# A two-layer hybrid decoder trunk on one core: memory queries produced already turned, and two output projections written in another order

## The chip, the cores and the metric

The kernel runs on one core of one Trainium2 chip. The metric is the time of one execution in microseconds (us) of device time.

## The reference, cut to what matters

256 positions of 1024 features pass through two layers. Each layer has a token mixer, a four-head cross-attention into 256 memory tokens, one output projection over both, and a SwiGLU feed-forward part (FFN) of inner width 2816, each behind an RMS norm:

```python
for i in range(2):
    h = rmsnorm(x, norm_mix[i]); mem_n = rmsnorm(mem, norm_mem[i])
    mix, mem_q = gmlp_mixer(h, ...) if i == 0 else nsa_mixer(h, ...)
    mem_o = mem_cross_attention(mem_q, mem_n, w_mem_kv[i])
    x = x + concatenate([mix, mem_o], -1) @ w_out[i]
    h = rmsnorm(x, norm_ffn[i])
    x = x + (silu(h @ wg) * (h @ wu)) @ wd
return rmsnorm(x, norm_final)

def mem_cross_attention(q, mem_n, w_kv):       # 4 heads of 64
    k, v = split(mem_n @ w_kv, 2)
    p = softmax(einsum('bshd,bmhd->bhsm', q, k) * 64 ** -0.5)
    return einsum('bhsm,bmhd->bshd', p, v)
```

Layer 0 is a gated spatial unit (`u * (w_s @ norm(v) + b)`, 12 groups). Layer 1 is a sparse attention of 12 heads with three gated branches: a compressed one (15 blocks), a selected one and a sliding one.

## The kernel before, in words

The 256 positions are two blocks `tb` of 128 rows. Every product in float32 is made of three matmuls (`mm3`, lines 229 to 231): activations and weights are each split into a high and a low part in a reduced float32, and high by high, low by high and high by low are added up in one PSUM bank. The weights stream in by DMA on the SP queue into three `raw` buffers (line 153); ACT casts the high part `wH` (L123), DVE subtracts for the low part `wL` (L124), seven buffers each. A raw buffer is loaded anew once the `wL` of its last piece is made. The same two lines split activations into `aH` and `aL`. A norm's factor per row (`rstd`) is not applied to the activations but behind the product, where it is evicted.

PE's order is written by hand. A model clock (`Flow`) advances by the length of each product, and side chains (generators that `spawn` starts and that `yield` delays) emit their transposes (L245) and small matmuls when the clock has reached them. A wait that the model clock doesn't foresee is not filled with other work: PE runs in order. ACT, DVE, POOL and the DMA queue are ordered by a scheduler with priorities; up to `early.close()` it orders them with a timeline simulation.

PSUM has four banks `mm` for projections and accumulators and four banks `tr` for transposes, scores and attention outputs. A tile named `tr` can be written only when the tile four requests earlier has been read.

*Layer 0.* Behind the gating products come, for each block, the memory queries (`WQ0`, 256 wide), scaled by `rstd` on DVE (L693) and turned by two transposes on PE (`mem_queries`, copy on L377). `mem_kv` makes the keys and values of the memory (`WK0`). Meanwhile `v_chain` makes the gated product `gm` (L673), turns it and splits it into k-tiles 0 to 5 of `mix`. `mem_attention` does for each block: scores (L389), maximum (L393, DVE), its negative scaled (`nb`, L395, POOL), four Exp (L401, ACT), division (L406, POOL), after a delay `MEMLAT` the transposes of the probabilities and their copies (L414, ACT), then the output (L422, 16 matmuls) that is split into k-tiles 6 and 7 of `mix`. The output projection (`down`) adds up k-tiles 0 to 3 of all four accumulators (two blocks, two halves), and once both memory attentions are done, 4 to 7.

*Layer 1.* Six pairs of heads `m` pass through `scores(m)` (L927 to L931; mask and row maximum on DVE, L947; eight Exp on ACT, L951; division on POOL, L956; the compressed branch's softmax in `pcx`, L961 to L967), `turn(m)` (12 transposes of probabilities, three `tr` tiles, copies on ACT, L976 and L982; then in a fourth `tr` tile the one transpose of `pcx`, copy on L985) and `attend(m)` (L1003, 32 matmuls into one `tr` tile, split into `aH`, `aL`). Between them `mixed((k, tb))` puts two products of the output projection, k-tile k of block tb. Per step m nine `tr` tiles are asked for: four by scores, four by turn, one by attend. Behind the last pieces the transposes of the new `x` (L245, `x`), their split and the FFN follow.

Of the kernel before, what the change touches and what calls it, by code (L numbers as in the profile page):

```python
# [12 lines left out]
ALU = mybir.AluOpType  # L13
# [3 lines left out]
SEQ = 256  # L17
# [6 lines left out]
SCALE = 0.125  # L24
# [35 lines left out]
HI = 150  # L60
UP = 500
MEMLAT = 9.0
# [6 lines left out]
def body(tc, t, out):  # L69
    nc = tc.nc  # L70
    PE, ACT, DVE, POOL, SP = nc.tensor, nc.scalar, nc.vector, nc.gpsimd, nc.sync
    with ExitStack() as ctx:
# [309 lines left out]
        def mem_attention(qTs, tb, kv, dst, done):  # L382
# [12 lines left out]
            POOL.tensor_scalar(nb, mx, -SCALE, None, op0=ALU.mult)  # L395
            sm = tiny([128, 4], "sm")
            parts = [small([128, 2, 256]) for _ in range(2)]
            for i in range(2):
                for j in range(2):
                    n = i * 2 + j  # L400
                    ACT.activation(parts[i][:, j, :], scs[i][:, j * 256 : (j + 1) * 256], AF.Exp, bias=nb[:, n : n + 1],  # L401
                                   scale=SCALE, accum_out=sm[:, n : n + 1])
# [247 lines left out]
        def v_chain():  # L650
# [17 lines left out]
            for c, n in ((0, 512), (512, 256)):  # L668
                for tb in range(2):
# [4 lines left out]
                    yield 1.0  # L674
# [12 lines left out]
        qT0 = [None, None]  # L687
        for tb in range(2):
            ps = mm()
            gemm(ps, n0.act, tb, WQ0, 256)  # L690
            mq = small([128, 256])
            with tc.high_priority(offset=HI):
                DVE.tensor_scalar(mq, ps[:, 0:256], n0.rstd[tb], None, op0=ALU.mult)  # L693
            flow.spawn(mem_queries(mq, tb, qT0), 1.2)
        flow.until(lambda: mem_done)
        kv0 = mem_kv(WK0)
        flow.until(lambda: None not in qT0)
        for tb in range(2):
            flow.spawn(mem_attention(qT0, tb, kv0, mix, mo_done), 1.0 + 5.5 * tb)
# [4 lines left out]
        down(accs, mix, [0, 1, 2, 3], WO0[0] + WO0[1], True, False)  # L704
        flow.until(lambda: len(mo_done) == 2)
        down(accs, mix, [4, 5, 6, 7], WO0[2] + WO0[3], False, True,
             lambda *a: flow.spawn(f0.chain(*a)))
# [262 lines left out]
        def turn(m):  # L970
# [12 lines left out]
            tc_ = tr()  # L983
            transposes(tc_, pcs[:, m % 2], 1)
            ACT.copy(pcT[:, m % 2], tc_[:, 0:128])  # L985
            turned[m] = pT0, pT1

# [30 lines left out]
        def step(f, *a):  # L1018
            with tc.high_priority(offset=UP if f is turn else HI):
                f(*a)  # L1020
# [30 lines left out]
        step(turn, 0)  # L1051
        step(scores, 2)
        step(attend, 0)
        step(turn, 1)
        mixed((0, 0))
        step(scores, 3)
        step(attend, 1)
        step(turn, 2)
        mixed((1, 0))
        step(scores, 4)  # L1060
        step(attend, 2)
        step(turn, 3)
        mixed((0, 1))
        step(scores, 5)
# [3 lines left out]
        mixed((1, 1), (3, 0))  # L1068
        step(attend, 4)
        step(turn, 5)  # L1070
        mixed((2, 1), (4, 0))
        step(attend, 5)
        mixed((3, 1), (5, 0), (4, 1), (5, 1))
# [66 lines left out]
```

## Time and profile before

| | |
|---|---|
| time, median of 3 runs | 633.94 us (633.56 to 634.37) |
| the profiled execution | 634.55 us, span 632.8 us |
| PE matmul busy | 618.1 us (98%) |
| DVE, ACT, POOL busy | 377.1, 327.3, 58.2 us |
| granted TensorE clock | 0.998 |
| HBM read | 108.07 MB, 172 GB/s over the span |

The busy share says how much of the span an engine worked. PE at 98% leaves some 15 us in which it did nothing, and the waits list says in front of which lines. In the timeline of PE the distance between the starts of neighbours is the true pace, since the ends of matmuls are modelled: 0.12 us for a matmul of 256 columns and 0.23 us for one of 512.

### The profile page before, as it was taken

The page shows a single profiled execution, that of the slowest core. Times are in us where ns is not written, and L with a number is a line of the kernel's source. Part 1 is how long each engine was busy: PE and PEld are TensorE (multiplying, and loading weights), DVE is VectorE, ACT ScalarE, POOL GpSimd, SP SyncE. Part 2 cuts the span into 40 slices and gives each one's busy share as a digit, 9 for nine tenths or more (in the row PEclk, how much of TensorE's full clock was granted, in tenths as well). Part 3 has the DMA queues.
Part 4 walks back from the last instruction along what each step waited for, and adds up shares of the span by engine and source line. Part 5 has one row for each costly group of instructions (what it writes and reads, how often), then busy time and mean ns, then how long its engine had stood idle before and what let it go on. Part 6 is the DMA issues. An engine that isn't in the chain of part 4 may idle for free.

```text
span 632.8 us, 8848 instructions
## 1 busy us (share of the span) xinstructions
PE 618.1 (98%) x3382; PEld 513.9 (81%) x3382; DVE 377.1 (60%) x616; ACT 327.3 (52%) x553; POOL 58.2 (9%) x90
## 2 busy tenths in 40 slices
PE   8999999999999999999999999899999999999995
PEld 7889879888888888889886787678988888888884
DVE  3998457464554544566688479766544645446344
ACT  4885557452534434456543559766533535344423
POOL 0330121000000000002001204431000000000001
PEclk9999999999999999999999999999999999999999
DMA  7966254555546464643967742133554655647401
GB/s 244 369 217 247 75 165 169 200 172 186 177 171 225 138 261 134 241 159 87 330 201 206 193 103 65 35 121 115 198 199 134 226 173 179 220 138 235 159 1 67
DMA packets 57331, 109.69 MB, mean 173 GB/s; under 512 B 3429, under 2 KB 19401, under 8 KB 57289
## 3 DMA queue, kind: packets, MB, share of 16 engines
q1 hardware_dynamic: 57272, 109.12, 51.9%
q8 instruction: 26, 0.43, 0.3%
q14 instruction: 17, 0.13, 0.1%
q10 hardware_dynamic: 16, 0.00, 0.0%
HBM read 108.07 MB, written 1.05 MB: 172 GB/s over the span
## 4 chain that ended last, share of the span: by engine, by line
PE 90%; ACT 5%; DVE 2%; DMA 1%; issue 1%; POOL 0%; SPq 0%; POOLq 0%; ACTq 0%; DVEq 0%
PE mm L229 14%; PE mm L230 14%; PE mm L231 14%; PE tr L230 13%; PE tr L231 13%; PE tr L229 13%; PE tr L245 5%; ACT mid L951 3%; PE tr L800 1%; DMA x<-in_x_dram 1%; PE tr L389 1%; PE tr L422 1%; PE tr L1003 1%; ACT wH L123 1%; DVE wL L124 0%
## 5 line engine op out<-in xcount | busy, mean ns | idle before, releaser
L124 DVE TENSOR_TENSOR wL<-raw,wH 128x1024 fp32r<-128x1024 f32 (+1 forms) x170 | 205.5, 1228 | 149.5 <-ACT wH L123 143.8
L123 ACT CAST wH<-raw 128x1024 fp32r<-128x1024 f32 (+1 forms) x170 | 173.8, 1043 | 152.3 <-PE tr L230 75.5
L229 PE MATMUL tr<-wH,aH 128*128 128x512 f32 (+1 forms) x384 | 143.8, 375 | 0.0
L230 PE MATMUL tr<-wH,aL 128*128 128x512 f32 (+1 forms) x384 | 142.8, 372 | 0.6 <-DVE aL L124 0.6
L231 PE MATMUL tr<-wL,aH 128*128 128x512 f32 (+1 forms) x384 | 142.7, 372 | 0.0
L229 PE MATMUL mm<-wH,aH 128*128 128x512 f32 (+2 forms) x224 | 87.7, 391 | 0.0
L230 PE MATMUL mm<-wH,aL 128*128 128x512 f32 (+2 forms) x224 | 83.2, 371 | 0.0
L231 PE MATMUL mm<-wL,aH 128*128 128x512 f32 (+2 forms) x224 | 83.2, 371 | 0.0
L230 PEld LDWEIGHTS tr<-wH,aL 128*128 128x128 f32 x384 | 72.4, 188 | 13.0 <-DVE aL L124 0.9
L231 PEld LDWEIGHTS tr<-wL,aH 128*128 128x128 f32 x384 | 72.3, 188 | 12.5
L229 PEld LDWEIGHTS tr<-wH,aH 128*128 128x128 f32 x384 | 72.3, 188 | 12.3
L229 PE MATMUL mm<-wH,mid 128*128 128x512 f32 (+1 forms) x208 | 79.2, 381 | 0.0
L230 PE MATMUL mm<-wH,mid 128*128 128x512 f32 (+1 forms) x208 | 77.9, 374 | 0.0
L231 PE MATMUL mm<-wL,mid 128*128 128x512 f32 (+1 forms) x208 | 77.8, 374 | 0.0
L229 PEld LDWEIGHTS mm<-wH,aH 128*128 128x128 f32 x224 | 42.9, 191 | 9.6 <-issue 4.0
L231 PEld LDWEIGHTS mm<-wL,aH 128*128 128x128 f32 x224 | 42.6, 190 | 7.4
L258 POOL TENSOR_SCALAR rstd<-ss 128x1 f32<-128x1 f32 x14 | 8.0, 575 | 434.6 <-ACT junk L250 430.5
L230 PEld LDWEIGHTS mm<-wH,aL 128*128 128x128 f32 x224 | 42.7, 191 | 5.6
L231 PEld LDWEIGHTS mm<-wL,mid 128*128 128x128 f32 x208 | 39.2, 188 | 7.1
L230 PEld LDWEIGHTS mm<-wH,mid 128*128 128x128 f32 x208 | 39.3, 189 | 6.8 <-DVE mid L124 0.5
L229 PEld LDWEIGHTS mm<-wH,mid 128*128 128x128 f32 x208 | 39.2, 189 | 6.7 <-ACT mid L123 0.4
L453 DVE SCALAR_TENSOR_TENSOR small<-tr,rstd,small 128x512 f32<-128x512 f32 (+1 forms) x24 | 16.9, 703 | 36.5 <-PE tr L231 36.5
(158 smaller groups left out, 652.6 us busy)
## 6 DMA issues: line engine op xcount, KB each, us to landing
raw<-in_ffn_w_down_dram SPq DMA_DIRECT2D x22, 1024.0 KB, 5.1
raw<-in_ffn_w_gate_dram SPq DMA_DIRECT2D x20, 1024.0 KB, 5.2
raw<-in_ffn_w_up_dram SPq DMA_DIRECT2D x20, 1024.0 KB, 5.1
raw<-in_nsa_w_in_dram SPq DMA_DIRECT2D x6, 1024.0 KB, 6.9
raw<-in_gmlp_w_in_dram SPq DMA_DIRECT2D x4, 1024.0 KB, 8.1
raw<-in_w_mem_kv_dram SPq DMA_DIRECT2D x4, 1024.0 KB, 5.8
raw<-in_gmlp_w_out_dram SPq DMA_DIRECT2D x4, 1024.0 KB, 6.2
raw<-in_nsa_w_out_dram SPq DMA_DIRECT2D x12, 256.0 KB, 4.9
```

Source lines behind the costliest of these rows:

```text
L123: ACT.copy(H, src)
L124: DVE.tensor_tensor(L, src, H.bitcast(F32), op=ALU.subtract)
L229: PE.matmul(ps, aH, bH, start=first, stop=False)
L230: PE.matmul(ps, aL, bH, start=False, stop=False)
L231: PE.matmul(ps, aH, bL, start=False, stop=last)
L245: PE.transpose(ps[:, (at + j) * 128 : (at + j + 1) * 128], src[:, j * 128 : (j + 1) * 128], ident)
L258: POOL.tensor_scalar(r, ss[:, 0:1], ss[:, 1:2], EPS, op0=ALU.add, op1=ALU.add)
L389: PE.matmul(scs[i][:, j * 256 : (j + 1) * 256], qT[r, j, :], kv[r, j, :], start=True, stop=True)
L422: PE.matmul(o[i * 64 : i * 64 + 64, blk(j)], kv[:, 2 + b, h : h + 64], pTs[i][:, j * 2 + b, :], start=b == 0, stop=b == 1)
L453: DVE.scalar_tensor_tensor(h, ps[:, :n], nrm.rstd[tb], sil[tb], op0=ALU.mult, op1=ALU.mult)
L800: PE.matmul(ph[s * 64 : s * 64 + 60, 0:256], X[s][:, k // 8, k % 8, :], w1[q, s][:, j, :], start=k == 0, stop=k == 15)
L951: ACT.activation(o, o, AF.Exp, bias=nb[:, i : i + 1], scale=-1.0, accum_out=sm[:, i : i + 1])
```

## The change

(a) Layer 0's memory queries are computed already turned: the weights `WQ0` are the stationary operand, and the activations of both blocks, 256 columns, move. One DVE copy (L696 of the changed kernel) evicts both blocks. The row factor is now missing in the queries; it goes into the scale of the Exp and of `nb`, as a `[128,1]` tile per block (`qs`, two tiny POOL operations each). The two scalings on L693, the four transposes and the two copies on L377 are gone. (b) `MEMLAT` is 8 for 9, the second memory attention is spawned 3.5 behind the first for 5.5, and `gm` is waited for 2.0 on the model clock for 1.0. (c) Layer 0's output projection runs k-tiles 4 and 5 of block 0 ahead of the point that asks for both memory attentions, then 6 and 7 of block 0, then 4 to 7 of block 1. (d) In layer 1 the transpose of the compressed branch is a step of its own, `turn_c`, put behind the next `mixed` for m = 1 to 5, and the last `mixed` pieces are in another order.

```diff
-MEMLAT = 9.0
+MEMLAT = 8.0
...
-            POOL.tensor_scalar(nb, mx, -SCALE, None, op0=ALU.mult)
+            POOL.tensor_scalar(nb, mx, -SCALE if scales is None else scales[tb][1], None, op0=ALU.mult)
...
                     ACT.activation(parts[i][:, j, :], scs[i][:, j * 256 : (j + 1) * 256], AF.Exp, bias=nb[:, n : n + 1],
-                                   scale=SCALE, accum_out=sm[:, n : n + 1])
+                                   scale=SCALE if scales is None else scales[tb][0], accum_out=sm[:, n : n + 1])
...
                     DVE.tensor_tensor(gm, U[:, tb, c : c + n], Vv[:, tb, c : c + n], op=ALU.mult)
-                    yield 1.0
+                    yield 2.0
...
-        qT0 = [None, None]
+        ps = mm()
+        for j in range(2):
+            for k in range(8):
+                aH, aL = n0.act
+                mm3(ps[:, j * 256 : (j + 1) * 256], WQ0[k](blk(j)), (aH[:, k, :], aL[:, k, :]), k == 0, k == 7)
+                if j == 1:
+                    WQ0[k].done()
+        qt = small([128, 2, SEQ])
+        DVE.tensor_copy(qt, ps.rearrange("p (j n) -> p j n", j=2))
+        qT0, scales = [qt[:, :, blk(tb)] for tb in range(2)], []
         for tb in range(2):
-            ps = mm()
-            gemm(ps, n0.act, tb, WQ0, 256)
-            mq = small([128, 256])
-            with tc.high_priority(offset=HI):
-                DVE.tensor_scalar(mq, ps[:, 0:256], n0.rstd[tb], None, op0=ALU.mult)
-            flow.spawn(mem_queries(mq, tb, qT0), 1.2)
+            up, dn = tiny([128, 1], "qs"), tiny([128, 1], "qs")
+            POOL.tensor_scalar(up, n0.rstd[tb], SCALE, None, op0=ALU.mult)
+            POOL.tensor_scalar(dn, n0.rstd[tb], -SCALE, None, op0=ALU.mult)
+            scales.append((up, dn))
         flow.until(lambda: mem_done)
         kv0 = mem_kv(WK0)
-        flow.until(lambda: None not in qT0)
         for tb in range(2):
-            flow.spawn(mem_attention(qT0, tb, kv0, mix, mo_done), 1.0 + 5.5 * tb)
+            flow.spawn(mem_attention(qT0, tb, kv0, mix, mo_done, scales), 1.0 + 3.5 * tb)
...
         down(accs, mix, [0, 1, 2, 3], WO0[0] + WO0[1], True, False)
+        down(accs, mix, [4, 5], WO0[2], False, False, None, (0,))
         flow.until(lambda: len(mo_done) == 2)
-        down(accs, mix, [4, 5, 6, 7], WO0[2] + WO0[3], False, True,
-             lambda *a: flow.spawn(f0.chain(*a)))
+        after = lambda *a: flow.spawn(f0.chain(*a))
+        down(accs, mix, [6, 7], WO0[3], False, True, after, (0,))
+        down(accs, mix, [4, 5, 6, 7], WO0[2] + WO0[3], False, True, after, (1,))
...
-            tc_ = tr()
-            transposes(tc_, pcs[:, m % 2], 1)
-            ACT.copy(pcT[:, m % 2], tc_[:, 0:128])
             turned[m] = pT0, pT1
+        def turn_c(m):
+            t = tr()
+            transposes(t, pcs[:, m % 2], 1)
+            ACT.copy(pcT[:, m % 2], t[:, 0:128])
...
         step(turn, 2)
         mixed((1, 0))
+        step(turn_c, 2)
         step(scores, 4)
...
-        mixed((1, 1), (3, 0))
+        mixed((1, 1))
+        step(turn_c, 4)
+        mixed((3, 0))
         step(attend, 4)
         step(turn, 5)
-        mixed((2, 1), (4, 0))
+        mixed((2, 1))
+        step(turn_c, 5)
         step(attend, 5)
-        mixed((3, 1), (5, 0), (4, 1), (5, 1))
+        mixed((4, 0), (5, 0), (3, 1), (4, 1), (5, 1))
```

Three places show how instructions move. On DVE, in layer 0's output projection, `raw` and `wL` are streamed weights, and `aL` is the low part of the memory attention's output (`tr`: its PSUM tile; `x`: the new residual). Before:

```order
L124 TENSOR_TENSOR wL_948<-raw_811,wH_947 128x1024
L124 TENSOR_TENSOR aL_430<-tr_953,aH_429 128x2x128
L124 TENSOR_TENSOR wL_993<-raw_919,wH_992 128x1024
L124 TENSOR_TENSOR aL_430<-tr_978,aH_429 128x2x128
L307 TENSOR_TENSOR x_92<-mm_821,x_92 128x512
```

With the change:

```order
L124 TENSOR_TENSOR wL_952<-raw_928,wH_951 128x1024
L124 TENSOR_TENSOR aL_430<-tr_974,aH_429 128x2x128
L124 TENSOR_TENSOR aL_430<-tr_991,aH_429 128x2x128
L307 TENSOR_TENSOR x_92<-mm_816,x_92 128x512
```

The first block's `aL` now stands behind a streamed weight whose raw tile (`raw_928`) has a late load; before, one `aL` stood ahead of that weight (`raw_919` there). ACT's casts stand in the same order.

On PE, at the same place, from the transposes of the second block's probabilities (`small`) to the first products behind both attentions. Before:

```order
L422 MATMUL tr<-small,memkv 64x128 x8
L245 MATMUL tr<-ident,small 128x128 x8
L422 MATMUL tr<-small,memkv 64x128 x8
L229 MATMUL mm<-wH,aH 128x512
L230 MATMUL mm<-wH,aL 128x512
```

With the change:

```order
L245 MATMUL tr<-ident,small 128x128 x8
L422 MATMUL tr<-small,memkv 64x128 x8
L229 MATMUL mm<-wH,aH 128x512
L230 MATMUL mm<-wH,aL 128x512
L231 MATMUL mm<-wL,aH 128x512
L229 MATMUL mm<-wH,aH 128x512
```

The second block's transposes used to stand between the two outputs (L422); now two products stand there, and the transposes are ahead of the first output.

On PE in layer 1, the end of a `turn` (`mid`: probabilities), the compressed branch's transpose (`pcx`) and one `mixed`. Before:

```order
L245 MATMUL tr<-ident,mid_3535 128x128 x4
L245 MATMUL tr<-ident,mid_3552 128x128 x4
L245 MATMUL tr<-ident,pcx 128x128
L229 MATMUL mm<-wH,aH 128x512
L230 MATMUL mm<-wH,aL 128x512
L231 MATMUL mm<-wL,aH 128x512
```

With the change:

```order
L245 MATMUL tr<-ident,mid_3547 128x128 x4
L229 MATMUL mm<-wH,aH 128x512
L230 MATMUL mm<-wH,aL 128x512
L231 MATMUL mm<-wL,aH 128x512
L229 MATMUL mm<-wH,aH 128x512
L230 MATMUL mm<-wH,aL 128x512
L231 MATMUL mm<-wL,aH 128x512
L245 MATMUL tr<-ident,pcx 128x128
L936 MATMUL tr<-KT,QT 128x271 x2
```

The single transpose went from ahead of the two products to behind them, right before the next scores.

## Rows read from the trace of the kernel before

**Rows 1.** Busy time of PE, its weight loads, DVE, ACT and POOL in layer 1's attention. Columns: window in us, its length, busy times with instruction counts, granted TensorE clock, DMA share, GB/s.

```profile
378.00:440.00 62.00, 57.52 (x456) 43.47 (x453) 46.48 (x194) 47.34 (x151) 21.16 (x26) 1.00 0.26 86
```

**Rows 2.** The longest of the waits of PE: line, what it waited for, us in total, times, longest.

```profile
PE tr L245 <- DVE aL L124: 2.5, 3, 1.0
```

**Rows 3.** Timeline of PE while the memory's keys are made: start in us, duration, what, and in brackets the idle time before it and its releaser.

```profile
56.94 0.28 PE L231 MATMUL mm<-mid,wH 128*128 128x256 f32 x1
57.43 0.85 PE L245 MATMUL tr<-ident,small 128*128 128x128 f32 x6 [0.21 <-DVE small L673]
...
60.94 0.28 PE L231 MATMUL mm<-mid,wH 128*128 128x256 f32 x1
61.06 0.38 PE L245 MATMUL tr<-ident,small 128*128 128x128 f32 x2
...
61.39 0.28 PE L230 MATMUL mm<-mid,wL 128*128 128x256 f32 x1
```

**Rows 4.** Timeline of PE at the memory attention's end in layer 0.

```profile
82.21 1.03 PE L245 MATMUL tr<-ident,small 128*128 128x128 f32 x8
83.00 0.48 PE L229 MATMUL mm<-wH,aH 128*128 128x512 f32 x1
...
83.55 0.40 PE L231 MATMUL mm<-wL,aH 128*128 128x512 f32 x1
84.09 1.57 PE L422 MATMUL tr<-small,memkv 128*64 128x128 f32 x16
85.60 1.09 PE L245 MATMUL tr<-ident,small 128*128 128x128 f32 x8
86.93 1.58 PE L422 MATMUL tr<-small,memkv 128*64 128x128 f32 x16 [0.24 <-ACT small L414]
88.43 0.50 PE L229 MATMUL mm<-wH,aH 128*128 128x512 f32 x1
```

**Rows 5.** Timeline of PE in layer 1's attention: the transposes of `turn` (x12), the compressed branch's (pcx) and the first matmul of scores (L927).

```profile
387.36 1.48 PE L245 MATMUL tr<-ident,mid 128*128 128x128 f32 x12
388.67 0.27 PE L245 MATMUL tr<-ident,pcx 128*128 128x128 f32 x1
...
393.86 1.53 PE L245 MATMUL tr<-ident,mid 128*128 128x128 f32 x12
395.94 0.33 PE L245 MATMUL tr<-ident,pcx 128*128 128x128 f32 x1 [0.55 <-ACT mid L976]
...
401.43 1.53 PE L245 MATMUL tr<-ident,mid 128*128 128x128 f32 x12
403.95 0.33 PE L245 MATMUL tr<-ident,pcx 128*128 128x128 f32 x1 [0.99 <-DVE aL L124]
...
405.59 0.73 PE L927 MATMUL tr<-KT,QT 64*128 64x271 f32 x4
...
409.24 1.53 PE L245 MATMUL tr<-ident,mid 128*128 128x128 f32 x12
411.77 0.33 PE L245 MATMUL tr<-ident,pcx 128*128 128x128 f32 x1 [1.00 <-DVE aL L124]
...
413.42 0.73 PE L927 MATMUL tr<-KT,QT 64*128 64x271 f32 x4
...
418.63 1.53 PE L245 MATMUL tr<-ident,mid 128*128 128x128 f32 x12
420.63 0.33 PE L245 MATMUL tr<-ident,pcx 128*128 128x128 f32 x1 [0.48 <-DVE aL L124]
```

**Rows 6.** Timeline of DVE in the same stretch: the low part of attend's output.

```profile
411.30 0.41 DVE L124 TENSOR_TENSOR aL<-tr,aH 128x256 fp32r<-128x256 f32 x1
```

**Rows 7.** Timeline of ACT in the same stretch: the first of a step's eight Exp and, at the step's end, the copy of the compressed branch's transpose.

```profile
406.92 0.40 ACT L951 ACTIVATE mid<-mid,nb 128x128 f32<-128x128 f32 x1 [2.19 <-DVE nb L947]
...
412.27 0.27 ACT L985 COPY pcx<-tr 128x128 f32<-128x128 f32 x1
```

**Rows 8.** Timeline of PE at the start of layer 1's FFN.

```profile
438.52 0.28 PE L229 MATMUL tr<-wH,aH 128*128 128x256 f32 x1
439.37 0.39 PE L230 MATMUL tr<-wH,aL 128*128 128x256 f32 x1 [0.58 <-DVE aL L124]
```

**Rows 9.** Timeline of ACT in layer 0: the first Exp of the second block, and a weight's cast that waits for its load.

```profile
79.74 0.48 ACT L401 ACTIVATE small<-tr,nb 128x256 f32<-128x256 f32 x1 [3.19 <-POOL nb L395]
...
89.53 1.05 ACT L123 CAST wH<-raw 128x1024 fp32r<-128x1024 f32 x1 [2.17 <-DMA raw<-in_ffn_w_up_dram]
```

**Rows 10.** Timeline of POOL there: the two divisions of the first block.

```profile
76.91 2.04 POOL L406 TENSOR_TENSOR small<-small,rs 128x512 f32<-128x512 f32 x2 [2.33 <-DVE rs L404]
```

**Rows 11.** Timeline of the DMA queue there: the issue of that load and the next.

```profile
84.18 2.35 SPq L153 DMA_DIRECT2D raw<-in_ffn_w_up_dram  x2
```

**Rows 12.** Instructions on the `raw` tiles from 80 to 92 us (durations in ns: least, median, most; starts; the last line gives the loads' time from issue to landing).

```profile
L124 DVE TENSOR_TENSOR wL<-raw,wH x4: 1214/1368/2057, 82.6 to 90.6; 128x1024 fp32r<-128x1024 f32 x4
...
DMA to landing us min/median/max: 4.7/5.3/6.1
```

**Rows 13.** From the list of DMA issues, the slow end: tile and source, count, KB each, median us to landing.

```profile
wsr<-in_gmlp_w_s_dram SPq DMA_DIRECT2D x1, 768.0 KB, 11.3
```

**Rows 14.** One line of the source, L250 (no per-row scale): durations in ns.

```profile
L250 ACT ACTIVATE junk<-x x18: 612/630/633, 17.1 to 626.9; 128x512 bf16<-128x512 f32 x18
```

**Rows 15.** Timeline of ACT: an activation as large whose scale is a per-row tile.

```profile
50.71 0.68 ACT L613 ACTIVATE U<-mm,rstd 128x512 f32<-128x512 f32 x1
```

More of the change, by code (lines that the diff above doesn't have):

```diff
@@ L380, in mem_queries, with mem_attention @@
             yield
-        def mem_attention(qTs, tb, kv, dst, done):
+        def mem_attention(qTs, tb, kv, dst, done, scales=None):
             qT = qTs[tb]
@@ L1018, in step @@
         def step(f, *a):
-            with tc.high_priority(offset=UP if f is turn else HI):
+            with tc.high_priority(offset=UP if f in (turn, turn_c) else HI):
                 f(*a)
@@ L1051, in body @@
         step(turn, 0)
+        step(turn_c, 0)
         step(scores, 2)
@@ L1055, in body @@
         mixed((0, 0))
+        step(turn_c, 1)
         step(scores, 3)
@@ L1063, in body @@
         mixed((0, 1))
+        step(turn_c, 3)
         step(scores, 5)
```

## The prediction

> **What bounds the kernel now.** First the busy time by stretch: in layer 1's attention PE, at the full granted clock (1.00), works 57.52 of 62 us, while DVE and ACT work 46.48 and 47.34 [rows 1]. So PE sets the time, also in this stage, and a change is worth what it removes from PE's row of work plus the holes that it closes there, less the holes that it opens. Then PE's waits: the longest entry is three waits for `aL`, 2.5 us in all, in front of a transpose [rows 2]. Then PE's timeline around each hole. There I take the distance between starts, not the bracketed idle time, because it is what the next matmul really lost.
>
> **What closes.** (1) Four transposes of the queries go. Two of them stand between two matmuls that start 0.45 us apart, where 0.24 would be two steps of 0.12 [rows 3]: 0.21 for two, **0.42** for four. The scalings and copies on DVE that go with them are off PE's path, and the one new copy has all of the memory's key product ahead of its reader: nothing.
>
> (2) In front of the six transposes that hold the first `gm`, PE loses 0.49 − 0.12 = **0.37** [rows 3]; the releaser is the `gm` product. With the scalings gone and the delay of 2.0, `gm` is made during the query product and asked for seven products into the memory's keys. I take all of it; the other end is nothing.
>
> (3) In the memory attention the second block's transposes of probabilities are followed by its output 1.33 us later, where eight such transposes with no wait behind them take 0.79; the bracket shows 0.24 for it [rows 4]. The copy of the transposes (ACT) is awaited. I take 0.45, between the two. In front of the first output 0.54 pass behind one matmul, where 83.00 to 83.55 is 0.55 for two [rows 4]; of the 0.27 over I take 0.2. Now two products or a whole block's work stand between transposes and output, so **0.65** goes.
>
> (4) The large one. With nothing in the way the 12 transposes of `turn` take 1.31 us to the next instruction; in the four later steps it is 2.08, 2.52, 2.53 and 2.00 [rows 5]. That is 0.77 + 1.21 + 1.22 + 0.69 = **3.89**. The single transpose asks for the PSUM bank in which `attend` has just written, and this is free only when DVE has made `aL`: at 411.30 + 0.41 = 411.71, and PE goes on at 411.77 [rows 5, 6]. Moved behind the two products, these cover it: from the transpose to the next scores 403.95 to 405.59 pass, 1.64 us [rows 5], and the longest of the holes is 1.22.
>
> (5) At the FFN's start the second matmul comes 0.85 us behind the first instead of 0.12: `aL` of the new x is late [rows 8], **0.73**. In the new order four products (12 matmuls of 512 columns, at 0.23, twice the 0.12 of 256 columns [rows 3]: 2.76 us) lie between the transposes of the last half and the FFN instead of two. It goes.
>
> Together 0.42 + 0.37 + 0.65 + 3.89 + 0.73 = 6.06 us.
>
> **What opens.** (6) In layer 0, `aL` of the first block now stands on DVE behind a weight's low part, and on ACT `aH` stands behind its cast; that cast waits for a load. Queued behind it are both blocks' `aH` and `aL`, and PE waits for them. PE: it began behind both outputs at 88.43 [rows 4]; (1) to (3) take 1.44 off, and four products (2.76) are now ahead of that point: 89.75, and the matmul that reads `aL` is the second one, 90.0. The other side: before, the second block's Exp began at 79.74, waiting for `nb` [rows 9]. Now its scores come earlier, but POOL works in order and ends the first block's divisions at 76.91 + 2.04 − 0.79 = 78.16 [rows 10]; with `nb`, an estimated 0.25, the Exp begins at 78.4, 1.3 earlier. The load is issued behind a low part that follows these Exp: 84.18 − 1.3 = 82.9 [rows 11]. Before, its cast began 5.35 us after the issue [rows 9, 11], so 88.2 now; a cast of 1.05, a low part of 1.2 at least [rows 12] and `aL` of 0.41 [rows 6] make 90.9. Each of the eight Exp now has a second per-row operand. No row shows two; an activation of 512 columns with one takes 0.68, without 0.63 [rows 14, 15], so 0.05 each, 0.4 in all: 91.3. PE stands for **1.3**. With the fastest and slowest of the loads there, 4.7 and 6.1 us [rows 12], 0.65 and 2.05.
>
> Beside this the Trainium skill ("ScalarE: Activation LUTs", section "What ACT_TABLE_LOAD costs") says that each [128,1] pointer operand adds about 93 ns to an ACTIVATE. It speaks against this part of the change; by it, as an estimate, eight Exp would be 0.74 longer, PE would stand for 1.65, and the sum would be 0.35 smaller. The trace's difference agrees in sign and is about half as large.
>
> (7) In layer 1 the bank that the single transpose no longer asks for goes to the next request. Three places come out late: `attend(1)`, whose bank is one of scores(3) and is free when DVE has masked them; the last scores of m = 5, whose bank waits for the copy of `turn_c(3)` behind a weight's cast on ACT; `attend(5)`, which reads the copy of `turn_c(5)`, also behind a cast. None of these waits is in the trace. A cast there is about 1.05 long [rows 9], so each may cost between nothing and 1.0, which is also the largest such wait now [rows 5]. I take 0.6, 0.45 and 0.6, the middle, since the products in front cover about half: **1.65**.
>
> (8) At nothing: the turned projection has as many matmuls of as many columns, and PE runs the memory's keys, where weights are the stationary operand too, at 0.12 a matmul [rows 3]. The four POOL operations on `qs` lie early, where POOL waits. The output projection of layer 0 does the same products in another order; its later pieces cover the split of block 0's new x. The shorter `MEMLAT` in layer 1 moves one group of transposes by one product. If their covers failed, each would cost what one transposition wait costs, 0.2 to 0.5.
>
> Sum: 6.06 − 1.3 − 1.65 = 3.1 us gained. The profiled execution, 634.55, becomes 631.45; it lies 0.61 above the median of 633.94, from which I forecast **630.8**. This kernel's measurement can tell about 0.2%, 1.27 us, from no change, so "same" is 632.67 to 635.21.
>
> **The rivals.** *Everything is covered.* The new waits of (6) and (7) don't come, because loads land early and the scheduler's casts fall into gaps: 633.94 − 6.06 = 627.9. For it: ACT and DVE idle a quarter of the stage [rows 1]. Against it: the cast already waits 2.17 for its load [rows 9].
>
> *The softmax chain takes it back.* A step of layer 1 takes 413.42 − 405.59 = 7.83 us on PE [rows 5]. ACT works from its first Exp at 406.92 to the copy that ends at 412.54 [rows 7], 5.6, and a weight's cast of 1.05 besides: 6.7 of it. If PE shortens to 6.6, ACT is as long, and a step whose Exp wait for DVE (2.19 now [rows 7]) can't become shorter than that chain. In the worst case (4) comes back whole in front of scores or attend: 6.06 − 3.89 − 1.3 = 0.87, so 633.1. Against it: before the Exp ACT stands idle, so the chain has slack.
>
> *Slower.* The load in (6) is the one mechanism with a large price. PE stands as long as it is late, one to one. If it lands as slowly as the slowest row, 11.3 us [rows 13], 5.95 later than 5.35, PE stands 7.25 and the sum is 6.06 − 1.65 − 7.25 = −2.84: 636.8. The change breaks even at a landing of 8.5 us and is slower by over 1.27 from 9.7. For it: the cast is now ahead of `aL` on both engines, so nothing else shields PE. Against it: 4.7 to 6.1 was the range there [rows 12], and the slow row is a far larger load at the start, among many.
>
> That the change doesn't do what it says can't be, but for the waits: in PE's order the four transposes are gone and the single ones stand behind the products.
>
> **How the numbers follow.** The forecast, with new waits between half and all of the bounds, has 0.66; all covered 0.13; the chain 0.15; slower 0.06. The range goes from 628.5 (the fastest load, 0.65, and none of (7): 6.06 − 0.65 = 5.4) to 633.1 (the chain; about as much comes from the slowest load and 1.0 in each place of (7): 6.06 − 2.05 − 3.0 = 1.0). Faster by over 0.2%: the forecast, all covered and a quarter of the chain's case, 0.83; within 0.2%: 0.11; slower: 0.06.
>
> **What would show it.** (1) three groups of transposes instead of five in the stretch of the memory's keys; (2), (3) no wait in front of those transposes and outputs; (4) 12 transposes followed by a product after 1.3 to 1.4 us in each step; (5) 0.12 between the first two FFN matmuls; (6) a wait of 0.6 to 2 us of a product's second matmul for `aL` near 90 us, with a cast before it that waits for its load; (7) waits of up to 1 us in front of scores and attend. The forecast is wrong if (4)'s time appears again in front of scores or attend, if (6) is over 4 us, or if steps of layer 1 stay near 7.8 us.

## The result and the profile after

The changed kernel takes 629.43 us (median of 4, 629.09 to 630.8) against 633.75 (4 runs of the kernel before): a ratio of 0.9936 (95% interval 0.9918 to 0.9955), 4.3 us faster. Forecast were 630.8, 3.1 faster, with a range of 628.5 to 633.1. The profiled execution is 629.09 us with a span of 627.4.

Where the time went shows best if PE's timeline is cut at six instructions that stand in both programs, since PE works 98% of the span in both. The numbers are differences of their starts, in us:

| stretch of PE | before | before, again | changed | changed, again |
|---|---|---|---|---|
| start to the transpose of the 92 constant rows (head) | 22.16 | 20.67 | 20.43 | 20.47 |
| to the memory's keys (query product in it) | 33.82 | 33.79 | 33.59 | 33.58 |
| memory's keys and values, `gm` turned | 13.42 | 14.57 | 12.80 | 12.81 |
| memory attention, output projection, to layer 0's FFN | 31.50 | 31.49 | 31.10 | 31.62 |
| FFN, layer 1's products, to turn(0) | 286.46 | 286.08 | 285.83 | 285.92 |
| turn(0) to the third matmul of layer 1's FFN | 52.23 | 52.24 | 50.37 | 50.34 |
| to the end | 193.21 | 193.26 | 193.28 | 193.26 |

The large and exact gain is layer 1's, 1.87 us; the forecast gave it 3.0. Layer 0's stretches differ by 0.23 + 0.62 + 0.40 = 1.25, where the forecast had 0.1. The rest of the difference between the two first profiles is 1.73 in the head, where the change moves nothing, and 0.63 in the stretch from layer 0's FFN to turn(0) (both below).

The waits of PE in the changed kernel (line, releaser: us in all, times, longest). The 2.5 us of [rows 2] are gone, and a new entry stands in their place:

```profile
PE mm L230 <- DVE aL L124: 1.4, 3, 0.7
```

It is a product's second matmul that waits for `aL`, once in layer 0 and twice in layer 1.

PE's timeline in the memory's keys, which answers to [rows 3]: start, duration, what.

```profile
56.42 0.29 PE L231 MATMUL mm<-mid,wH 128*128 128x256 f32 x1
56.54 0.60 PE L245 MATMUL tr<-ident,small 128*128 128x128 f32 x4
...
59.48 0.60 PE L245 MATMUL tr<-ident,small 128*128 128x128 f32 x4
...
62.44 0.38 PE L245 MATMUL tr<-ident,small 128*128 128x128 f32 x2
```

Four groups of transposes are left, all of `gm` (the fourth, of two, at 65.17), and the first follows 0.12 us behind its neighbour, where 0.49 had passed. (1) and (2) together are worth 0.23 + 0.62 = 0.85 here, for 0.79.

PE's timeline from the second block's transposes to the first product that reads both attentions, which answers to [rows 4]:

```profile
82.66 1.03 PE L245 MATMUL tr<-ident,small 128*128 128x128 f32 x8
83.62 1.09 PE L422 MATMUL tr<-small,memkv 128*64 128x128 f32 x16
84.64 0.50 PE L229 MATMUL mm<-wH,aH 128*128 128x512 f32 x1
...
86.23 1.09 PE L422 MATMUL tr<-small,memkv 128*64 128x128 f32 x16
87.26 0.49 PE L229 MATMUL mm<-wH,aH 128*128 128x512 f32 x1
88.41 0.50 PE L230 MATMUL mm<-wH,aL 128*128 128x512 f32 x1 [0.66 <-DVE aL L124]
```

Two things are to be seen. The 16 matmuls of an output now take 1.02 to the next instruction, twice; before they took 1.51 and 1.50 [rows 4]. And the wait (6) is there: 1.15 between the first two matmuls of a product instead of 0.34, so 0.81.

What the outputs waited for in the kernel before shows on ACT and in the weight loads (PEld) that belong to these matmuls:

```profile
83.43 1.09 ACT L414 COPY small<-tr 128x512 f32<-128x512 f32 x2
84.09 0.19 PEld L422 LDWEIGHTS tr<-small,memkv 128*64 128x64 f32 x2 [0.58 <-ACT small L414]
84.58 0.85 PEld L422 LDWEIGHTS tr<-small,memkv 128*64 128x64 f32 x14 [0.30 <-ACT small L414]
```

The first two matmuls read the first copy of the turned probabilities, the third reads the second copy: 83.43 + 1.09 is 84.52, and the third starts at 84.58.

The same place on ACT, with one Exp, and on the DMA queue, which answer to [rows 9] and [rows 11]:

```profile
77.15 0.56 ACT L401 ACTIVATE small<-tr,nb,qs 128x256 f32<-128x256 f32 x1 [2.64 <-POOL nb L395]
...
85.72 1.05 ACT L123 CAST wH<-raw 128x1024 fp32r<-128x1024 f32 x1 [1.35 <-DMA raw<-in_ffn_w_up_dram]
```

```profile
81.89 2.35 SPq L153 DMA_DIRECT2D raw<-in_ffn_w_up_dram  x2
```

The cast that stands ahead of `aH` waits for its load, as forecast. The load took 3.83 us from issue to cast, not 5.35. Each Exp takes 0.56 instead of 0.47.

PE's timeline in layer 1, which answers to [rows 5]: turn(1), turn(2), turn(3), scores(5), attend(5).

```profile
390.24 1.53 PE L245 MATMUL tr<-ident,mid 128*128 128x128 f32 x12
391.85 0.50 PE L229 MATMUL mm<-wH,aH 128*128 128x512 f32 x1
392.65 0.50 PE L230 MATMUL mm<-wH,aL 128*128 128x512 f32 x1 [0.30 <-DVE aL L124]
...
397.76 1.53 PE L245 MATMUL tr<-ident,mid 128*128 128x128 f32 x12
399.37 0.50 PE L229 MATMUL mm<-wH,aH 128*128 128x512 f32 x1
400.29 0.50 PE L230 MATMUL mm<-wH,aL 128*128 128x512 f32 x1 [0.42 <-DVE aL L124]
...
401.75 0.73 PE L936 MATMUL tr<-KT,QT 64*128 64x271 f32 x4
...
405.40 1.53 PE L245 MATMUL tr<-ident,mid 128*128 128x128 f32 x12
406.69 0.48 PE L229 MATMUL mm<-wH,aH 128*128 128x512 f32 x1
...
408.37 0.73 PE L936 MATMUL tr<-KT,QT 64*128 64x271 f32 x4
...
409.07 1.75 PE L940 MATMUL tr<-KT,QT 64*128 64x512 f32 x4
...
424.46 0.44 PE L1014 MATMUL tr<-pcx,vc 128*64 128x128 f32 x4 [0.36 <-ACT pcx L997]
```

In step 3 the product follows the 12 transposes after 1.29 us, as forecast, and from turn to scores it is 2.97 instead of 4.18. In steps 1 and 2 it follows after 1.61, and its second matmul comes 0.80 and 0.92 later instead of 0.31 to 0.34: from turn to scores 3.99 in step 2, where 4.16 had been. What they wait for is on ACT:

```profile
391.44 0.35 ACT L123 CAST aH<-tr 128x256 fp32r<-128x256 f32 x1
```

and on DVE:

```profile
392.18 0.41 DVE L124 TENSOR_TENSOR aL<-tr,aH 128x256 fp32r<-128x256 f32 x1
```

391.44 + 0.35 is 391.79, and the product starts at 391.85; 392.18 + 0.41 is 392.59, and its second matmul starts at 392.65. The products behind turn(1) and turn(2) are (0,0) and (1,0): they read the very tile that attend(0) and attend(1) have just made.

The start of layer 1's FFN, which answers to [rows 8]:

```profile
433.79 0.28 PE L229 MATMUL tr<-wH,aH 128*128 128x256 f32 x1
433.90 0.38 PE L230 MATMUL tr<-wH,aL 128*128 128x256 f32 x1
```

0.11 instead of 0.85: (5) came whole.

### The profile page after: what moved, and what is told of

Its sections match the earlier page's. It is cut to its first block, busy times and chain, and to the rows that moved or that the text cites. A ratio compares the mean times of both kernels' runs of the same rounds, so it can differ in the third digit from the quotient of the medians.

```text
span 627.4 us, 8840 instructions
## 1 busy us (share of the span) xinstructions
PE 615.1 (98%) x3378; PEld 511.2 (81%) x3378; DVE 374.1 (60%) x613; ACT 328.7 (52%) x553; POOL 60.1 (10%) x94
## 4 chain that ended last, share of the span: by engine, by line
PE 89%; ACT 4%; DVE 2%; DMA 2%; issue 1%; POOL 1%; SPq 0%; POOLq 0%; ACTq 0%; DVEq 0%
PE mm L230 14%; PE mm L229 14%; PE mm L231 14%; PE tr L230 13%; PE tr L229 13%; PE tr L231 13%; PE tr L245 5%; ACT mid L960 2%; PE tr L1014 1%; DVE wL L124 1%; PE tr L809 1%; DMA x<-in_x_dram 1%; ACT wH L123 1%; ACT small L401 1%; DMA raw<-in_ffn_w_up_dram 1%
## 5 line engine op out<-in xcount | busy, mean ns | idle before, releaser
L229 PE MATMUL mm<-wH,aH 128*128 128x512 f32 (+2 forms) x208 | 82.1, 395 | 0.1
L230 PE MATMUL mm<-wH,aL 128*128 128x512 f32 (+2 forms) x208 | 78.6, 378 | 1.4 <-DVE aL L124 1.4
L231 PE MATMUL mm<-wL,aH 128*128 128x512 f32 (+2 forms) x208 | 78.3, 376 | 0.0
L229 PEld LDWEIGHTS mm<-wH,aH 128*128 128x128 f32 x208 | 39.2, 188 | 10.2 <-issue 3.8
L230 PEld LDWEIGHTS mm<-wH,aL 128*128 128x128 f32 x208 | 39.2, 189 | 8.0 <-DVE aL L124 2.6
L231 PEld LDWEIGHTS mm<-wL,aH 128*128 128x128 f32 x208 | 39.1, 188 | 7.6 <-DVE wL L129 0.5
```

Source lines behind the costliest of these rows:

```text
L229: PE.matmul(ps, aH, bH, start=first, stop=False)
L230: PE.matmul(ps, aL, bH, start=False, stop=False)
L231: PE.matmul(ps, aH, bL, start=False, stop=last)
```

## The experiments

The theory after the two traces: layer 1's gain is halved because two of the four products that should cover the wait for `aL` read that `aL` themselves; layer 0 gains more than forecast because the outputs hid a wait inside their 16 matmuls, and loses what the late load costs. The rival for layer 1 is the softmax chain on ACT, DVE and POOL, for layer 0 the forecast's own sum. All ratios are to the kernel before on the same chip.

**Halves of the change.** The first kernel, `l0_only`, is the changed one with layer 1's `turn` and order as before; the second, `l1_only`, is the kernel before with only these changed. Two places of the first one's edit:

```diff
-        step(turn_c, 1)
-        mixed((4, 0), (5, 0), (3, 1), (4, 1), (5, 1))
+        mixed((3, 1), (5, 0), (4, 1), (5, 1))
```

> The change without its layer-1 attention part: turned queries, delays and the first output projection as changed, the transposes of the compressed branch and the last products as before. From the trace of the changed kernel (theory): 0.2 + 0.6 in the memory's keys, 0.4 net at the output projection, 0.6 at layer 1's memory attention, together 1.8 us faster than before, about 632.0, with a wait of about 0.8 for aL behind the cast that waits for its load. The prediction's own terms (rival) give 1.44 - 1.3 = 0.1 for this part, about 633.6. A second rival: the first 20 us, which were 1.7 us shorter in the changed kernel's execution, are shortened by this part; then the first product behind the head comes at 20.4 here in every execution, and never in a kernel without this part.

631.43 us (5 runs), ratio 0.9966 (0.9954 to 0.9979).

> Layer 1's part alone: turn_c split off and moved, the last products reordered; layer 0 as before. Theory: the closed holes of four steps come back in part, because the products behind turn(1) and turn(2) read the tile that attend has just made; 1.9 us faster, about 631.9, steps 1 and 2 near 7.5 us, steps 3 and 4 near 6.6. The prediction's own terms (rival) give 3.89 + 0.73 - 1.65 = 3.0, about 630.8, with 12 transposes followed by a product after 1.3 us in all steps.

631.50 us (6 runs), ratio 0.9964 (0.9952 to 0.9976). The two medians lie 2.25 and 2.18 us below before; they add up to 4.4, the whole change. Layer 1's half takes 50.36 us from turn(0) to the FFN, as in the changed kernel, and this stretch refutes the forecast's 3.0 for it. Layer 0's half takes 0.26 + 0.61 + 0.01 off its three stretches (the load took 4.28 us there, and PE stood 1.29 for it). The median of layer 0's half is 1.4 lower than this accounts for, that of layer 1's half 0.3 (the end of this section comes back to it). My 0.6 at layer 1's memory attention does not hold: the stretch from layer 0's FFN to turn(0) is 285.99 in layer 0's half, 286.09 in the other and 286.08 in the second profile of before. The 286.46 of the first holds one loss of 0.45 in front of four transposes of layer 1's memory attention; half_swap, early_tb1 and shift (below) lose 0.3 to 0.35 at the same place, the others 0.15 or less.

**The Exp's scale as a constant.**

```diff
-                                   scale=SCALE if scales is None else scales[tb][0], accum_out=sm[:, n : n + 1])
+                                   scale=SCALE, accum_out=sm[:, n : n + 1])
```

The factor of `nb` (L395) becomes a constant in the same way, so that the queries' row factor is in neither.

> The changed kernel with the Exp's scale and the factor of nb in layer 0 as a constant again: the row factor of the queries is left out. Theory: each Exp of layer 0 takes 0.47 instead of 0.56 us, the second block's last Exp ends 0.7 us earlier, so does the load's issue, and the wait for aL at the first output projection falls from 0.8 to 0.1 us; 0.7 us faster than the changed kernel. Rival: the load's landing sets the wait, and PE waits 0.8 as before.

628.55 us (4 runs), ratio 0.9920 (0.9906 to 0.9934); the interval overlaps the changed kernel's, so the trace has to decide. The Exp take 0.47 again; relative to PE's arrival at the waiting matmul the load goes out 6.58 us ahead instead of 5.71. But it took 4.82 to the cast, and PE stood 0.94. Neither theory alone: the shorter Exp give 0.87 of lead, and the landing takes 0.99 of it back. One sum fits the eight profiles that have the changed kernel's order at this place: wait = issue + landing + 2.69 − arrival, where landing runs to the cast's start, arrival is when the second matmul would have come, and 2.69 is set from the changed kernel (cast, low part, `aL`):

| kernel | issue | landing | arrival | sum | PE stood |
|---|---|---|---|---|---|
| swap_latec (below) | 82.01 | 3.75 | 87.67 | 0.78 | 0.78 |
| changed | 81.89 | 3.83 | 87.60 | 0.81 | 0.81 |
| half_swap (below) | 81.64 | 3.84 | 87.33 | 0.84 | 0.85 |
| l0_only | 81.82 | 4.28 | 87.50 | 1.29 | 1.29 |
| changed, again | 81.92 | 4.40 | 87.59 | 1.42 | 1.43 |
| imm_scale | 81.11 | 4.82 | 87.69 | 0.93 | 0.94 |
| swap (below) | 82.17 | 4.88 | 87.82 | 1.92 | 1.92 |
| shift (below) | 82.25 | 4.91 | 87.92 | 1.93 | 1.93 |

So PE pays for the landing one to one, as the forecast's slower rival had it; landings of 3.75 to 4.91 us kept it between 0.78 and 1.93.

**Two products ahead of the late load.** `halves` is a new argument of `down`.

```diff
         down(accs, mix, [4, 5], WO0[2], False, False, None, (0,))
+        down(accs, mix, [4, 5], WO0[2], False, False, None, (1,), (0,))
```

> The changed kernel with k-tiles 4 and 5 of the second block's first half put between the two memory attentions of layer 0: two products, 1.4 us, ahead of the first product that reads aL. Theory: PE reaches that product 1.4 us later, and its wait is what issue + landing + 2.7 us leaves over: none for a landing of up to 4.4 us, 0.5 for 4.9. So 0.8 to 1.4 us faster than the changed kernel. Rival: with two products less behind block 0's last product the transposes of x or the FFN's first product wait for block 0's aL, and the gain is lost there.

628.86 us (6 runs), ratio 0.9928 (0.9915 to 0.9941); the interval overlaps the changed kernel's. The load took 4.17 us (81.07 to 85.24), PE does not wait for `aL` there, as the sum says (−0.17), and the stretch to layer 0's FFN takes 30.12 instead of 31.10 to 31.62. The rival's price shows too: behind the first products of the FFN a group of transposes of x is reached 0.32 us later than in the changed kernel (its bracket, 0.16, shows half of it). That leaves 0.7 to 1.2 of the 0.8 to 1.4 expected.

**Layer 1's products one place later.**

```diff
-        mixed((6, 1), (7, 1))
+        mixed((6, 1))
         step(turn, 0)
...
         step(turn, 1)
-        mixed((0, 0))
+        mixed((7, 1))
...
         step(turn, 2)
-        mixed((1, 0))
+        mixed((0, 0))
```

> The changed kernel with the products of layer 1 one place later: product (7,1) stands behind turn(1), (0,0) behind turn(2), (1,0) behind turn(3), (0,1) behind scores(5), (2,0) behind turn_c(4), (3,0) among the last. So no product directly behind a turn reads what attend has just made. Theory: in steps 1 and 2 the product follows the 12 transposes after 1.3 us and its second matmul does not wait, 0.8 + 0.9 = 1.7 us less there, minus up to 0.7 where turn(0) now has one product less in front; 1.0 to 1.7 us faster than the changed kernel. Rival: what PE waits for is the softmax chain on ACT (the cast of attend's output stands behind eight Exp), and the wait goes over to the next scores, turn or attend: no gain, steps 1 and 2 still 7.5 us.

631.36 us (5 runs), ratio 0.9962 (0.9949 to 0.9974); the median is 1.9 us above the changed kernel's, and in its profile the late load (table above) makes 0.5 to 1.0 of that. PE's timeline there, turn(1) and turn(2):

```profile
390.86 0.44 PE L245 MATMUL tr<-ident,mid 128*128 128x128 f32 x2
391.81 0.87 PE L245 MATMUL tr<-ident,mid 128*128 128x128 f32 x6 [0.51 <-POOL mid L965]
394.38 0.66 PE L245 MATMUL tr<-ident,mid 128*128 128x128 f32 x4 [1.69 <-POOL mid L965]
...
401.10 1.53 PE L245 MATMUL tr<-ident,mid 128*128 128x128 f32 x12
402.38 0.48 PE L229 MATMUL mm<-wH,aH 128*128 128x512 f32 x1
```

The dependence is shown: with another product behind it, turn(2) is followed after 1.28, and steps 2 and 3 take 6.89 and 6.62 us from scores to scores. But the product that moved had covered scores(1)'s softmax: turn(1) now waits 2.2 us for POOL. The stretch takes 52.96, with one more `mixed` in it (some 1.4 us) than in the changed kernel; counted from layer 0's FFN, where both have the same work, 337.80 stand against 336.20.

**Two products exchanged.** attend(m) makes both blocks of k-tile m, so (0,1) can stand behind turn(2).

```diff
         step(turn, 2)
-        mixed((1, 0))
+        mixed((0, 1))
...
         step(turn, 3)
-        mixed((0, 1))
+        mixed((1, 0))
```

> The changed kernel with two products of layer 1 exchanged: (0,1) now stands behind turn(2), (1,0) behind turn(3). attend(0) has made both blocks of k-tile 0, so the product behind turn(2) no longer reads the tile that was just made; nothing else moves. Theory: in step 2 the first product follows the 12 transposes after 1.3 instead of 1.6 us, its second matmul does not wait for aL, and the step from turn(2) to scores(4) takes 3.0 instead of 4.0 us; step 1 stays (1.6 and the wait). 0.9 us faster than the changed kernel. Rival: what waits is the softmax chain on ACT and DVE, which comes out at the next scores or attend; no gain.

630.61 us (6 runs), ratio 0.9952 (0.9938 to 0.9966); the stretch takes 50.33, no gain. PE behind turn(2):

```profile
399.06 1.53 PE L245 MATMUL tr<-ident,mid 128*128 128x128 f32 x12
400.34 0.48 PE L229 MATMUL mm<-wH,aH 128*128 128x512 f32 x1
...
402.02 0.73 PE L936 MATMUL tr<-KT,QT 64*128 64x271 f32 x4
...
402.72 1.75 PE L940 MATMUL tr<-KT,QT 64*128 64x512 f32 x4
405.06 0.66 PE L1014 MATMUL tr<-mid,V 128*64 128x128 f32 x8 [0.59 <-DVE pcx L954]
```

and DVE:

```profile
403.17 1.23 DVE L124 TENSOR_TENSOR wL<-raw,wH 128x1024 fp32r<-128x1024 f32 x1
404.31 0.28 DVE L956 CUSTOM_DVE_ANT_0 mid<-tr,causal 128x128 f32<-128x128 f32 x1
```

The hole behind turn(2) closed (2.96 for 3.99), and 1.3 us opened behind it: L940 takes 1.75 instead of 1.11, and attend(2) waits 0.59. That is what the rival foretold; the rows name the reason. (0,1) is the last reader of its weights; with it gone earlier, the next weight is split earlier, and its low part now stands on DVE in front of the masks of scores(4), which started 1.00 behind the scores' first matmul (L936) in the changed kernel (402.75 − 401.75) and start 2.29 behind it now (404.31 − 402.02). Further on, the last scores get back 0.64 and 0.40 opens behind turn(4), so the stretch comes out even.

**Halves of them exchanged.** The last reader of k-tile 0 stays behind turn(3).

```diff
         step(turn, 2)
-        mixed((1, 0))
+        mixed((0, 1, 0), (1, 0, 0))
...
         step(turn, 3)
-        mixed((0, 1))
+        mixed((0, 1, 1), (1, 0, 1))
```

> The changed kernel with halves of two products of layer 1 exchanged: behind turn(2) stand the first halves of (0,1) and (1,0), behind turn(3) their second halves, so that the weight piece of k-tile 0 is given back where the changed kernel gives it back, and ACT's and DVE's orders stay as they are. Theory (what ate the gain of the full exchange is the low part of a weight that moved ahead of the masks of scores(4) on DVE): here the masks keep their place, and the hole behind turn(2) shrinks from 0.9 to 0.2 us with nothing opening behind it; the stretch from turn(0) to the FFN of layer 1 takes 49.7 instead of 50.4 us. Rival (the softmax chain as a whole sets the pace of the first steps): the stretch stays at 50.3, and the wait comes out at scores(4) or attend(2).

629.08 us (5 runs), ratio 0.9934 (0.9921 to 0.9946). The stretch takes 49.66, 0.71 less, and nothing opens behind. PE's timeline there:

```profile
397.94 1.53 PE L245 MATMUL tr<-ident,mid 128*128 128x128 f32 x12
399.23 0.48 PE L229 MATMUL mm<-wH,aH 128*128 128x512 f32 x1
...
400.01 0.39 PE L229 MATMUL mm<-wH,aH 128*128 128x512 f32 x1
400.46 0.50 PE L230 MATMUL mm<-wH,aL 128*128 128x512 f32 x1
...
401.94 1.11 PE L940 MATMUL tr<-KT,QT 64*128 64x512 f32 x4
```

The first half covers `aH`, the second still loses 0.22 to `aL`, and L940 takes 1.11 again. On DVE the masks wait for PE once more, not PE for them:

```profile
402.23 0.29 DVE L956 CUSTOM_DVE_ANT_0 mid<-tr,causal 128x128 f32<-128x128 f32 x1 [0.30 <-PE tr L938]
```

The next weight's cast and low part are back behind the masks and the Exp of scores(4), and with them the 0.59 in front of attend(2) is gone. So the queue in front of the masks ate swap's gain at this place, not the length of the softmax chain, which has the same instructions in both.

**The compressed branch's transpose later.**

```diff
-        step(turn_c, 3)
         step(scores, 5)
+        step(turn_c, 3)
...
         step(turn_c, 5)
+        mixed((4, 0))
         step(attend, 5)
```

> As swap, and the compressed branch's transpose of m = 3 stands behind scores(5) instead of ahead of it, and product (4,0) stands between that of m = 5 and attend(5). Theory: scores(5) asks for no bank that waits for a copy behind a weight's cast, so its 1.7 us become 1.05; attend(5) no longer waits for the copy (1.0 us between its first and second group become 0.5). 1.2 us faster than swap, 2.1 faster than the changed kernel. Rival: the copy is late for attend(3) instead, which then waits about as long; no gain over swap.

637.61 us (6 runs), ratio 1.0067 (1.0055 to 1.0079). The edit does something else than was expected of it: m = 3 and m = 5 share one of the two slots of `pcx`, so this kernel turns the scores of m = 5 twice and m = 3's not at all, and the transpose waits for a whole softmax:

```profile
416.69 0.45 PE L245 MATMUL tr<-ident,pcx 128*128 128x128 f32 x1 [6.35 <-DVE pcx L976]
```

It tells nothing of the copy behind the cast. Its second part, (4,0) in front of attend(5), comes without the first in the next kernel.

**Three together, and two.** The first is half_swap, early_tb1 and (4,0) in front of attend(5); the second leaves the last of them out.

> half_swap, and product (4,0) between the compressed branch's transpose of m = 5 and attend(5), and the two products of early_tb1 between layer 0's memory attentions. Theory: the terms add: 0.7 behind turn(2), 0.5 at attend(5), 0.8 to 1.4 at the first output projection; 2.0 to 2.6 us faster than the changed kernel, the stretch from turn(0) to the FFN 49.2 us. Rival: the FFN's start waits instead, since one product less lies behind attend(5).

628.67 us (6 runs), ratio 0.9928 (0.9916 to 0.9940). The load took 4.49 us, the sum gives 0.11 and PE stood 0.12; that stretch takes 30.35. From turn(0) to the FFN it is 49.82, not 49.2. attend(5) no longer waits (0.49 for 1.02 between its first groups), but PE's timeline goes on:

```profile
426.06 0.50 PE L229 MATMUL mm<-wH,aH 128*128 128x512 f32 x1 [0.47 <-ACT aH L123]
```

That is (5,0), now directly behind attend(5), which makes what it reads: the mistake of step (4) once more, and the gain of 0.54 is gone.

> half_swap and early_tb1 together, without the product that was put in front of attend(5). Theory: both parts keep their own gain, since they lie in different stretches: from the memory's keys to layer 0's FFN 30.1 to 30.4 us (31.1 to 31.6 in the changed kernel, by the landing), from turn(0) to layer 1's FFN 49.7 (50.4): 1.4 to 2.1 us faster than the changed kernel, about 5.3 to 6 below before. Rival: the time lost to late landings and to the first 20 us hides it, and the ratio to before stays at 0.993.

627.89 us (5 runs), ratio 0.9922 (0.9908 to 0.9935), 30.13 and 49.68 us in its two stretches, both as expected; the 0.32 at the transposes of x is here too. Its median is the lowest here, but its interval overlaps the changed kernel's. That it is faster rests on the stretches: they are within 0.05 us of early_tb1's and half_swap's, and together they are 1.3 to 1.9 us shorter than the changed kernel's after the 0.32 is taken off.

**The kernels of before and after once more.**

> The kernel before once more, for one thing: where the first product behind the head starts. It was at 22.2 us in the two profiles that have layer 0 as before, and at 20.4 to 20.8 in the four with layer 0 changed, though nothing in those first 20 us is changed. If it is chance, it comes out between 20.4 and 22.3, most likely near 21.2, since the median of before lies 0.9 below its profiled execution; if it belongs to the kernel, at 22.2.

> The changed kernel once more, to see which parts repeat. From turn(0) to the FFN of layer 1 50.4 us, memory's keys 12.8 us as before; the first 20 us between 19.5 and 22.3, by chance; the wait at the first output projection as issue + landing + 2.7 us less PE's arrival.

633.78 and 629.71 us, one run each. The table above has their stretches. The head was 22.16, 20.67 and 22.32 us in the three profiles with layer 0 as before, and 19.5 to 20.8 in the eleven with it changed. In the first of them the matmuls of 512 columns come every 0.43 us up to 11.7 us and every 0.23 from 12.6 on; in the third a load of x is awaited for 1.67 us, and from 11 to 14 us the granted clock is 0.50, the lower of its two levels. So the longer heads go with PE at its lower rate for 3 to 4 us at the start, but swap too has matmuls every 0.43 us, from 7.7 to 9.8, and a head of 20.68. before_again shows that a long head does not belong to this program. In the first 19 us no engine's instructions differ between the two programs. Why two of three heads are long there and none of eleven here stays open.

In before_again the wait for `gm` differed as well:

```profile
57.06 0.85 PE L245 MATMUL tr<-ident,small 128*128 128x128 f32 x6 [1.36 <-DVE small L673]
```

It is 0.21 in [rows 3]. On DVE there stands in front of it:

```profile
54.16 0.69 DVE L643 TENSOR_TENSOR Vv<-tr,gT 128x512 f32<-128x512 f32 x1
54.76 1.22 DVE L124 TENSOR_TENSOR wL<-raw,wH 128x1024 fp32r<-128x1024 f32 x1
55.90 0.42 DVE L377 COPY small<-tr 128x256 f32<-128x256 f32 x1
56.23 0.68 DVE L673 TENSOR_TENSOR small<-U,Vv 128x512 f32<-128x512 f32 x1
```

These follow each other without a pause. PE begins the memory's keys 1.52 us earlier than in the first profile of before (54.46 and 55.98), but the product `gm` starts only 0.38 earlier (56.23 and 56.61), behind a weight's low part and behind the copy of the queries (L377), which the change takes away. So most of a shorter head is lost again in front of `gm`. From the start to the first product of the output projection the three profiles with layer 0 as before take 69.03 to 69.55 us, the eleven others 66.0 to 67.2: here the two kinds are apart in every profile.

With like heads nothing large is left over: between before_again and the second profile of the changed kernel, 4.1 us apart, the stretches give 0.20 + 0.21 + 1.76 − 0.13 + 0.16 + 1.90. Between the two first profiles the head takes the place of `gm`'s wait. How often each case comes in executions without a profile these runs do not show; the 1.4 us that layer 0's half gains beyond its stretches are of the size of either.

## Why the prediction was right, and where not

- (1), (2): right in mechanism, 0.79 forecast, 0.85 measured between the first profiles. But the pair at 61.06 in [rows 3] that gave (1) its price is `gm`'s; the queries' pairs stand in the query product (54.33) and at the end of the group at 57.43, and four groups are left where I wrote three. And (2) is mis-sized where the head is short: 1.5 in before_again.
- (3): mis-sized, 0.65 forecast. The stretch took 0.40 off in spite of 0.81 for (6), so 1.21 net. Most of it, 0.97, was a wait inside the 16 matmuls of the two outputs, 1.5 long where they need 1.02: the third matmul waited for the second copy on L414. I read the bracket in front of the group, and the group's own length not at all.
- (4): the step that failed is "moved behind the two products, these cover it". That held for turn(3) and turn(4). Behind turn(1) and turn(2) the products themselves read `aL`, and these steps, for which I had 0.77 + 1.21, gained 0.05 together (3.75 to 3.87 and 4.16 to 3.99). I followed the bank's releaser and not what the covering work reads. For turn(1) not even the releaser was `aL`: the bracket in [rows 5] names the copy on L976.
- (5): right, 0.73 forecast and 0.74 measured.
- (6): right in mechanism and place; 1.3 forecast, 0.81 and 1.43 in the two profiles of the changed kernel. That the size came out is luck: I had the load go out 6.7 us ahead of PE (90.0 − 83.3, with the 0.4 for the Exp) and land in 5.35; it went out 5.7 ahead and landed in 3.83 and 4.40. With 5.35 the sum would have given 2.3. Each Exp grew by 0.09, not 0.05; the Exp of layer 1's memory attention, whose scale stayed a constant, kept 0.47 in the same execution. I had compared two activations that differ in more than the operand: one reads SBUF, the other PSUM. The Trainium skill ("ScalarE: Activation LUTs", section "What ACT_TABLE_LOAD costs") says about 93 ns for each [128,1] pointer operand. The trace of this case agrees: 0.47 and 0.56.
- (7): of the three places attend(1) shows no wait; the last scores lost 0.64 (0.45 forecast), attend(5) 0.54 (0.6). Together 1.2 for 1.65.
- (8): nothing, as written: the stretch with the shorter `MEMLAT` in layer 1 changes by 0.2 or less between second profiles.

The sum came out near because errors of both signs met, and that is luck: layer 1 gave 1.1 less than forecast, layer 0's stretches 1.1 more in the first profiles, and some 1.2 us between the medians came from what no term priced, the head and the longer wait for `gm`. The rival "everything is covered" did not come; the slower rival's mechanism is real, but with layer 0 changed no landing reached 5 us. The chain did take part of (4) back, in the form of one cast and one subtraction that the products' own operands wait for.

## What to carry to other kernels

Before work is counted as cover for a wait, look at what it reads: a product that reads the late tile covers nothing. Compare a group's own length with the same group elsewhere: a wait inside it had no bracket in PE's row here, only in that of the weight loads. When work moves, look at the buffer that its last reader gives back: the next load or split moves with it, into somebody's queue.

## What the runs showed of the hardware

- One and the same load of 512 KB took 3.75 to 5.35 us from its issue to the start of the cast in fourteen profiles of nearly the same program. In the eight profiles with the order of the changed kernel PE's wait behind it is the sum above, 0.78 to 1.93 us.
- An Exp of 128x256 from PSUM took 0.47 us with a constant scale and 0.56 with a per-row tile as scale, its bias being a per-row tile in both.
- The head of one program differed by 1.5 us between two executions (22.16 and 20.67), with 512-column matmuls every 0.43 us up to 11.7 us in the first and every 0.23 from 10.9 on in the second. The row of the granted clock says 1.00 for the slow stretch of the first, and 0.50 from 11 to 14 us for a like stretch of l1_only.
